# RMSNorm and matmul on one core: tiles 112 to 115 stored as one transfer of four tiles

## The chip, the core and the metric

The kernel runs on one core of one Trainium2 chip. Its time is the device time in microseconds (us) of one launch, and the number compared is the median of several runs. The profile comes from one further execution, whose own time is given beside its span.

## The reference

```python
x: (16, 1024, 512) f32, gamma: (512,) f32, weight: (512, 768) f32
rms = np.sqrt(np.mean(x ** 2, axis=-1, keepdims=True) + eps)
x_norm = x / rms * gamma
return np.matmul(x_norm, weight)          # (16, 1024, 768) f32
```

Flattened, `x` has 16,384 rows (tokens) of 512 numbers and the output has 16,384 rows of 768. The output is 50.33 MB and `x` is 33.55 MB.

## The kernel before

**Tiles.** The tokens are cut into `NT` = 128 tiles of 128 tokens, one token to a partition. Beyond the first 32 tiles the tokens are dealt out so that partition p of a block of 32 tiles holds 32 tokens that follow one another in memory (`rows`, lines 140 to 143). A store of n such tiles therefore writes, for each partition, one run of n x 3,072 bytes: 3,072 bytes for one tile, 9,216 for three, 12,288 for four, 24,576 for eight.

**A tile's way.** `x` is loaded in blocks of 8 tiles (2 MB), cast to bf16 by POOL (L190, L255), turned so that features lie on partitions (PE transposes at L226 and DVE copies at L236; DVE 32 by 32 transposes at L266 for four tiles out of every 16), multiplied by the weights, which already hold gamma (L302, eight matmuls to a tile), and scaled by 1/rms as it leaves PSUM for the buffer `ot`: even tiles by ACT (L274), odd ones by DVE (L276). ACT also sums the squares (L198).

**Order.** `Order` records each operation with what it reads and writes, in program order, and then gives out waits and semaphores. A transfer takes a semaphore from a pool of free ones. The program order is written out by hand in the loop over pairs of tiles (line 420 on).

**Stores.** `ot` has room for 32 tiles. `o_first` and `o_size` (line 138) say which tiles go out together: 4, 4, 8, 8, 8 for the first 32 tiles, then eights, and for the last 32 tiles 8, 8, 1, 3, 4, 4, 3, 1. `finish_tile` calls `store` after each tile; `store` issues a transfer, on SP's queue (line 295), when the tile is the last of its stretch. A stretch whose first tile stands in `DIVIDED` (tile 112 alone) is sent as two transfers, of partitions 0 to 59 and 60 to 127 (`PARTS`). The very last store, of tile 127, is issued by SP after a no-op, while ACT waits for the stores ahead of it (lines 454 to 464).

**What waits for a store.** A slot of `ot` is written again 32 tiles later, so nothing in the kernel writes over tiles 96 to 127 once they are scaled. Their stores are waited for at the end of the program alone. The loads of `x` are issued `LEAD` = 14 pairs ahead, and by the time tile 112 is scaled all of them have landed: after that only stores move.

Of the kernel before, what the change touches and what calls it, by code (L numbers as in the profile page):

```python
# [16 lines left out]
P = 128  # L17
# [83 lines left out]
def kernel(  # L101
# [20 lines left out]
    NT = N // P  # L122
    NP = NT // 2
    XG, RING = 16, 32
# [3 lines left out]
    def stretches(*sizes):  # L128
        first, size, i = {}, {}, 0
        for n in sum(sizes, []):  # L130
            for t in range(i, i + n):
                first[t], size[t] = i, n
            i += n
        assert i == NT
        return first, size

    x_first, x_size = stretches([4, 4, 8, 8, 8], *[[8, 8, 8, 8]] * (NT // RING - 1))
    o_first, o_size = stretches([4, 4, 8, 8, 8], *[[8, 8, 8, 8]] * (NT // RING - 2), [8, 8, 1, 3, 4, 4, 3, 1])

    def rows(ap, i, n):  # L140
        t = 4 if i < 8 else 8 if i < XG else XG if i < RING else RING
        base = i - i % t
        return ap[base * P:(base + t) * P, :].rearrange("(p t) d -> p t d", t=t)[:, i - base:i - base + n, :]
# [26 lines left out]
    def cells(name, slot, i, n=1):  # L170
        return [(name, slot, t) for t in range(i, i + n)]
# [108 lines left out]
    def accumulator():  # L280
        return next(turns) % 3

    DIVIDED = (NT - XG,)
    PARTS = [slice(60), slice(60, P)]

    def store(i):
        first, n = o_first[i], o_size[i]
        if i == first + n - 1:
            at = first % RING
            src, dst = ot[:, at:at + n, :], rows(out, first, n)  # L290
            for part in PARTS if first in DIVIDED else [slice(0, P)]:
                store_rows(dst[part], src[part], cells("ot", 0, at, n) + ([("ot", 1, at + n - 1)] if i == NT - 1 else []))

    def store_rows(dst, src, of):
        order.transfer(SP, lambda: SP.dma_start(out=dst, in_=src), reads=of)
# [23 lines left out]
    def finish_tile(i, a, engine):  # L319
        at = i % RING  # L320

        r = rstd[:, i:i + 1]
        if i == NT - 1:
            for half, by, lo, hi in ((0, ACT, 0, WIDE), (1, DVE, WIDE, O)):
                scale(by, ot[:, at, lo:hi], ops[a][:, lo:hi], r, [("ops", a, half), ("rstd", i)], [("ot", half, at)])
        else:
            before = [("ot", 0, at - 1)] if i == o_first[i] + o_size[i] - 1 and o_size[i] > 1 else []
            scale(engine, ot[:, at, :], ops[a][:, :O], r,
                  [("ops", a, 0), ("ops", a, 1), ("rstd", i)] + before, [("ot", 0, at)] + (opening if i == OPEN else []))
        store(i)  # L330
# [169 lines left out]
```

## The time before, and its profile

| What | Value |
|---|---|
| Median of 3 runs | 208.66 us (208.47 to 208.71) |
| The profiled execution's own time | 208.44 us |
| Its span, first to last instruction | 206.3 us |
| PE busy | 194.7 us, 94% of the span |
| DVE, ACT, POOL busy | 148.4, 145.1, 60.4 us |
| Read from and written to memory | 35.13 MB and 50.33 MB, 414 GB/s over the span |
| Queue 1 (SP: all stores, early loads) | 60.29 MB |
| Queue 10 (ACT: later loads) | 25.17 MB |
| Last matmul ends | about 197.4 us |
| Last store issued | 198.34 us |

The span is measured from the first to the last instruction of the program. The profiled execution took 2.1 us more than its span, and 0.22 us less than the median of the timed runs. An engine of the chip that computes (PE, DVE, ACT, POOL) is told apart from the 16 DMA engines that move the data; the profile's DMA row is the mean busy share of those 16.

### The profile page before, as it was taken

Reading aid. Unit: us, or ns where it says so; the run is one execution under the profiler, and the core shown is the slowest. Engines: PE = TensorE matmul, PEld = TensorE weight load, DVE = VectorE, ACT = ScalarE, POOL = GpSimd, SP = SyncE. Lnnn points to the kernel's source line nnn. Section 1 sums busy time; section 2 is a strip of 40 time slices with the busy share of each in tenths; the row PEclk is TensorE's granted clock in tenths of the full one; section 3 lists DMA queues with packets and bytes.
Section 4 is the critical chain, followed back from the end, with each engine's and each line's share of the span. In section 5 each row is a group of like instructions: output and inputs, shape, how many; then the busy total and the mean of one; then the engine's idle time right before and its main releaser. Section 6 shows DMA issues by size and latency. Waiting matters only on the chain.

```text
span 206.3 us, 2788 instructions
## 1 busy us (share of the span) xinstructions
PE 194.7 (94%) x1240; PEld 72.4 (35%) x717; DVE 148.4 (72%) x254; ACT 145.1 (70%) x345; POOL 60.4 (29%) x36
## 2 busy tenths in 40 slices
PE   7898999999999999999999999999999999999920
PEld 1233443342443333433343333433333334433200
DVE  0445647998579966999579975999569974999500
ACT  2789898877777687777787687677877687663330
POOL 1447733154206430153305170060704215000000
PEclk9999999999999999999999999999999999999985
DMA  6999999999999999999999999999999999999993
GB/s 211 419 438 445 391 392 436 424 447 419 437 424 438 429 427 427 426 442 429 429 429 424 446 426 435 419 422 446 434 429 424 427 432 446 429 415 410 422 421 135
DMA packets 5779, 85.62 MB, mean 415 GB/s; under 512 B 645, under 2 KB 647, under 8 KB 1159
## 3 DMA queue, kind: packets, MB, share of 16 engines
q1 hardware_dynamic: 4035, 60.29, 69.0%
q10 hardware_dynamic: 1732, 25.17, 28.6%
q8 instruction: 7, 0.11, 0.2%
q14 instruction: 5, 0.04, 0.0%
HBM read 35.13 MB, written 50.33 MB: 414 GB/s over the span
## 4 chain that ended last, share of the span: by engine, by line
PE 87%; DMA 7%; SPq 1%; POOL 1%; ACT 0%; issue 0%
PE ps L302 77%; PE ps L226 10%; DMA xt<-in_x_dram 7%; POOL xb L190 1%; SPq L179 1%; SPq L352 0%; ACT ot L274 0%; SPq L495 0%; SPq L454 0%
## 5 line engine op out<-in xcount | busy, mean ns | idle before, releaser
L302 PE MATMUL ps<-w_bf,xT 128*128 128x512 bf16 (+1 forms) x800 | 147.2, 326 | 0.0
L274 ACT ACTIVATE ot<-ps,rstd 128x768 f32<-128x768 f32 (+1 forms) x65 | 58.4, 898 | 47.1 <-PE ps L302 46.1
L198 ACT ACTIVATE jk<-xt 128x512 bf16<-128x512 f32 x128 | 78.7, 619 | 3.0 <-DMA xt<-in_x_dram 3.0
L190 POOL CAST xb<-xt 128x2048 bf16<-128x2048 f32 (+3 forms) x23 | 46.7, 2044 | 105.6 <-PE ps L226 61.7
L276 DVE TENSOR_SCALAR ot<-ps,rstd 128x768 f32<-128x768 f32 x64 | 64.3, 1005 | 10.5 <-PE ps L302 9.1
L298 PEld LDWEIGHTS <-xT 128*128 128x128 bf16 x400 | 39.2, 98 | 58.3 <-issue 57.4
L226 PE MATMUL ps<-ident_f,xb 128*128 128x128 f32 x200 | 54.0, 274 | 1.4 <-POOL xb L190 1.1
L236 DVE COPY xT<-ps 128x1024 bf16<-128x1024 bf16 (+1 forms) x52 | 34.2, 658 | 29.4 <-PE ps L226 28.7
L266 DVE STREAM_TRANSPOSE xTq<-xq 32x256 f32<-32x256 f32 x112 | 48.8, 435 | 1.9
L226 PEld LDWEIGHTS ps<-ident_f,xb 128*128 128x128 f32 x200 | 28.0, 141 | 47.9 <-issue 43.2
L302 PE MATMUL ps<-w_bf,xTq 128*128 128x512 bf16 x224 | 42.8, 326 | 0.0
L198 ACT ACTIVATION_READ_ACCUMULATOR jk<-xt 128x1 f32 x128 | 24.4, 191 | 0.0
L298 PEld LDWEIGHTS <-xTq 128*128 128x128 bf16 x112 | 11.0, 98 | 14.5 <-issue 14.5
L255 POOL CAST xq<-xt 128x2048 bf16<-128x2048 f32 x7 | 13.3, 1897 | 6.1 <-DVE xTq L266 6.1
L302 PE MATMUL ps<-ot 128*128 128x512 bf16 x14 | 5.1, 514 | 1.4 <-DVE ot L360 1.4
L203 ACT ACTIVATE ssq<-ssq,eps_sb 128x8 f32<-128x8 f32 (+3 forms) x20 | 6.0, 299 | 0.5
L205 DVE RECIPROCAL rstd<-ssq 128x8 f32<-128x8 f32 (+3 forms) x20 | 3.7, 191 | 2.7 <-ACT ssq L203 2.7
L274 ACT ACTIVATE w_bf<-ot,g_sb 128x768 bf16<-128x768 f32 x2 | 1.9, 936 | 0.8 <-DMA ot<-in_weight_dram 0.8
L384 DVE COPY g_sb<-ps 128x4 f32<-128x4 f32 x1 | 0.2, 163 | 3.1 <-PE ps L378 3.1
L348 ACT ACT_TABLE_LOAD x1 | 1.3, 1283 | 1.5 <-SPq L454 1.5
L276 DVE TENSOR_SCALAR w_bf<-ot,g_sb 128x512 bf16<-128x512 f32 (+2 forms) x3 | 1.4, 495 | 0.9 <-DMA ot<-in_weight_dram 0.9
L378 PEld LDWEIGHTS ps<-ident_f,ot 2*128 2x128 f32 x2 | 0.3, 200 | 2.6 <-issue 2.6
(11 smaller groups left out, 2.5 us busy)
## 6 DMA issues: line engine op xcount, KB each, us to landing
out_dram<-ot SPq DMA_DIRECT2D x13, 3072.0 KB, 23.2
xt<-in_x_dram ACTq DMA_DIRECT2D x12, 2048.0 KB, 19.2
xt<-in_x_dram SPq DMA_DIRECT2D x3, 2048.0 KB, 18.2
out_dram<-ot SPq DMA_DIRECT2D x4, 1536.0 KB, 9.3
out_dram<-ot SPq DMA_DIRECT2D x2, 1152.0 KB, 9.5
xt<-in_x_dram SPq DMA_DIRECT2D x2, 1024.0 KB, 7.3
ot<-in_weight_dram SPq DMA_DIRECT2D x2, 768.0 KB, 6.3
out_dram<-ot SPq DMA_DIRECT2D x1, 384.0 KB, 7.1
```

The costliest lines, as they stand in the source:

```text
L190: run(POOL, lambda: POOL.tensor_copy(out=xb[s][:, i % 8:i % 8 + n, :], in_=src), of, cells("xb", s, i % 8, n))
L198: run(ACT, lambda: ACT.activation(out=jk[n], in_=src[:, 0, :], func=AF.Square, accum_out=ssq[:, i:i + 1]), of, [("jk", n), ("ssq", i)])
L203: run(ACT, lambda: ACT.activation(out=ssq[:, s], in_=ssq[:, s], func=AF.Sqrt, scale=1.0 / D, bias=eps_sb), [("ssq", t) for t in range(i, i ...
L205: run(DVE, lambda: DVE.reciprocal(out=rstd[:, s], in_=ssq[:, s]), [("rms", i)], [("rstd", t) for t in range(i, i + n)])
L226: run(PE, lambda: PE.transpose(out=tp[b][:, t, h, :], in_=words[:, lo:lo + P], identity=ident_f), cells("xb", s, j % 4 * 2 + t) + ["ident" ...
L236: run(engine, lambda: copy(out=dst[:, t:t + n, :], in_=src[:, t:t + n, :]), [("tp", b)], cells("xT", j % XTS, t, n))
L255: run(POOL, lambda: POOL.tensor_copy(out=xq, in_=src), of, ["xq"])
L266: run(DVE, lambda: DVE.transpose(out=dst, in_=src), ["xq"], [("xTq", n)])
L274: run(ACT, lambda: ACT.mul(out=dst, in_=src, mul=r), reads, writes)
L276: run(DVE, lambda: DVE.tensor_single_scalar(out=dst, in_=src, scalar=r, op=mybir.AluOpType.mult), reads, writes)
L298: run(PE, lambda: PE.ldweights(lhsT), of)
L302: run(PE, lambda: PE.add_instruction(mybir.InstMatmult(name=nc.get_next_instruction_name(), engine=mybir.EngineType.PE, ins=[PE.lower_ap(r ...
```

## The change

Tile 112 joins tiles 113 to 115 in one stretch, and the division by partitions is gone. Where three transfers were issued for these four tiles (60 partitions of tile 112; 68 partitions of tile 112; tiles 113 to 115 on all partitions), one is issued (tiles 112 to 115 on all partitions), after tile 115. The bytes are the same. Nothing else of the kernel is touched.

```diff
-    o_first, o_size = stretches([4, 4, 8, 8, 8], *[[8, 8, 8, 8]] * (NT // RING - 2), [8, 8, 1, 3, 4, 4, 3, 1])
+    o_first, o_size = stretches([4, 4, 8, 8, 8], *[[8, 8, 8, 8]] * (NT // RING - 2), [8, 8, 4, 4, 4, 3, 1])
...
-    DIVIDED = (NT - XG,)
-    PARTS = [slice(60), slice(60, P)]
-
     def store(i):
         first, n = o_first[i], o_size[i]
         if i == first + n - 1:
             at = first % RING
             src, dst = ot[:, at:at + n, :], rows(out, first, n)
-            for part in PARTS if first in DIVIDED else [slice(0, P)]:
+            for part in [slice(0, P)]:
                 store_rows(dst[part], src[part], cells("ot", 0, at, n) + ([("ot", 1, at + n - 1)] if i == NT - 1 else []))
```

## The prediction

> **What bounds the kernel now.** I read the page's slices first. The DMA row stands at 9 from the second slice to the last but one, while PE goes quiet in the last two:
>
> ```profile
> PE   7898999999999999999999999999999999999920
> DMA  6999999999999999999999999999999999999993
> GB/s 211 419 438 445 391 392 436 424 447 419 437 424 438 429 427 427 426 442 429 429 429 424 446 426 435 419 422 446 434 429 424 427 432 446 429 415 410 422 421 135
> ```
>
> PE and the 16 DMA engines are both nearly full, so the end has to be looked at by itself. The chain of waits, cut to the end, stops at the scaling of tile 127 (197.45 us, 0.69 us long). The span goes on to 206.3 us. SP's own waits from 170 us on say what fills the rest:
>
> ```profile
> SPq L295 <- DVE ot L276: 25.2, 4, 10.7
> SPq L495 <- DMA out_dram<-ot: 6.7, 1, 6.7
> SPq L295 <- ACT ot L274: 4.2, 2, 3.4
> ```
>
> L495 is the program's end: it waits 6.7 us for a store. So the last 8 us belong to the stores. The table of stretches shows how (columns: stretch; its length; busy time of PE, PEld, DVE, ACT, POOL; PE clock; DMA share; GB/s):
>
> ```profile
> 187.00:193.00 6.00, 6.00 (x39) 1.76 (x18) 5.07 (x8) 1.80 (x2) 0.00 (x0) 1.00 0.99 415
> 193.00:198.00 5.00, 4.52 (x28) 1.27 (x13) 1.83 (x3) 2.35 (x3) 0.00 (x0) 1.00 0.97 413
> 198.00:202.00 4.00, 0.00 (x0) 0.00 (x0) 0.04 (x1) 0.13 (x1) 0.00 (x0) 0.71 0.99 414
> 202.00:203.20 1.20, 0.00 (x0) 0.00 (x0) 0.00 (x0) 0.00 (x0) 0.00 (x0) 0.50 0.51 207
> 203.20:204.70 1.50, 0.00 (x0) 0.00 (x0) 0.00 (x0) 0.00 (x0) 0.00 (x0) 0.50 0.17 70
> 204.70:206.30 1.60, 0.00 (x0) 0.00 (x0) 0.00 (x0) 0.00 (x0) 0.00 (x0) 0.50 0.01 4
> ```
>
> Full until 202 us, half at 202.6, then a share of 0.17 (three engines of 16) and less. The DMA engines don't end together; a few stragglers set the time, and a change that shifts bytes from one DMA engine to another shifts the end. The three stores that the change merges are three of the page's issues:
>
> ```profile
> out_dram<-ot SPq DMA_DIRECT2D x2, 1152.0 KB, 9.5
> out_dram<-ot SPq DMA_DIRECT2D x1, 384.0 KB, 7.1
> out_dram<-ot SPq DMA_DIRECT2D x1, 204.0 KB
> out_dram<-ot SPq DMA_DIRECT2D x1, 180.0 KB, 14.0
> ```
>
> (one of the two of 1152 KB, and those of 180 and 204 KB.)
>
> To see single engines I went to the trace's landing records. Each DMA engine that takes part in a store adds one to the store's semaphore when its share is down, so a store of all 16 shows 16 times. An engine works its stores off in order, so its landings can be strung together: each lies one share's time behind its landing of the store before.
>
> - Store of 60 rows: one count at 177.98, right at issue, then 15 landings, 187.66 to 191.42. Each lies 0.46 to 0.49 us behind one of the 16 landings of tiles 104 to 111; the landing at 187.99 alone has no follower. So 15 engines carry 4 rows each and one carries none.
> - Store of 68 rows: 12 counts at 178.34, right at issue, then four landings (189.65, 189.72, 191.11, 191.20). Each lies 1.98 to 1.99 us behind a landing of the 60-row store: four engines carry 17 rows each.
>
> The last of the 16 throughout is one engine; I call it X. Its landings beside those of the latest 17-row engine, and of a plain one that never ran dry (us):
>
> ```
> store (tiles)      104-111   60 rows  68 rows  113-115  116-119  120-123  124-126  127
> X                  190.96    191.42   -        194.25   198.01   201.72   204.49   205.41
> 17-row engine      188.75    189.22   191.20   193.95   197.61   201.30   204.02   204.95
> plain engine       189.11    189.58   -        192.32   195.95   199.60   202.36   203.30
> ```
>
> X is the only one that is slower all along: its share of an eight-tile store takes 7.54 us (183.42 to 190.96), where the earliest engine's takes 7.30 (179.89 to 187.19). It takes part in the 60 rows (its 191.42) and not in the 68. It never runs dry: its steps between the last stores, 3.76, 3.71, 2.77 and 0.92 us, are the time of its bytes. The span ends 0.9 us after its last landing.
>
> **The change part by part.**
>
> Bytes per engine. Now X writes 4 rows of 3,072 bytes and 8 of 9,216; afterwards 8 rows of 12,288. That is 12,288 bytes more. The shape after the change is in the trace already, in the two stores behind it (116 to 119, 120 to 123): X needs 3.76 and 3.71 us. What they replace is 0.46 + 2.83 = 3.29 us. The cost is +0.42 to +0.47 us; I take the middle, +0.44. The plain engine confirms it: 3.63 to 3.65 less 0.47 + 2.74 is +0.42 to +0.44. X has no idle time in any step behind this store, so all of it reaches the end: last landing 205.41 + 0.44 = 205.85.
>
> The 17-row engines are relieved. The latest now takes 0.47 + 1.98 + 2.75 = 5.20 us for the four tiles, and would take 3.66: -1.54 us, so it lands last at 203.41. Off the path, because X is later. The plain engines get the same +0.44 and end by 203.74. The engine left out of both parts gets 8 rows more, about 0.9 us, but it ran dry later (its landings of 116-119 and 120-123 lie 4.14 us apart, where 3.65 is work) and ends at 202.35 now; even with all of it, 203.25.
>
> Time of issue. Tile 112's bytes are issued at 182.53 instead of 177.46 and 177.89. What covers this is the eight-tile store ahead, which keeps the first engine busy to 186.8 (its landing, 187.19, less some 0.4 from the last packet's end to its landing). From issue to first packet, an engine that had run dry needed 0.84 us (120-123: issued 193.40, first packet 194.24), so the new transfer is ready at 183.4, 3.4 us ahead. Cost nothing; without the cover it would be up to 5 us on an idle engine.
>
> Issues and waits. SP loses two issues, 0.39 and 0.28 us, and one wait for ACT's tile 112. Its next issue waits for DVE's tile 115 until 182.5 anyway: nothing gained. No wait is added: the merged store waits where the three-tile store waits now. PE, ACT, DVE and POOL keep their instructions, and no slot of `ot` is reused. Per transfer an engine also writes its count, a packet of 0.009 us, one fewer for X; the landing steps already hold it.
>
> A rule of the Trainium skill speaks for the change: "DMA: Bandwidth & Descriptors", section "Rules for kernel authors", says that splitting a transfer by partitions is not worth it, since both halves spray over all 16 engines, and asks for one transfer of 128 partitions. By it the sum would be 0 or slightly below. The trace doesn't bear it out for this split: 15 and 4 landings, not 16 and 16. The same page's rule for the number of engines (section "Why a DMA increments its semaphore by 16 and not by 1": the largest number up to 16 that divides the rows) gives 15 for 60 and 4 for 68, as traced.
>
> **Sum**: +0.44 against the profiled execution, 208.44 to 208.88; the median of the runs is 0.22 higher, so 208.66 + 0.44 = 209.10.
>
> **The rivals.**
>
> 1. *Faster: a 17-row engine sets the end.* If X lands early in the runs that are not profiled, the 17-row engine at 204.95 is last. Without its 17 rows the end falls to the plain engines' 203.74: -1.21 us, 207.45. It decides when X lands before 204.51 (204.95 less 0.44), 0.9 us earlier than traced. For it: X's lead in lateness over that engine is only 0.46 us. Against: X is slower packet after packet over the whole trace, and the timed runs are no shorter than the profiled one, while they would be without X.
>
> 2. *No change: X runs dry first.* Four engines idled some 0.5 us ahead of the store issued at 193.40, and an engine that idles swallows the extra. X would have to be about 3.5 us earlier there (its share of 116-119 lands at 198.01, those four land at 194.07 to 194.39). Time 208.66.
>
> 3. *The last engine is the one left out of both parts.* Then it gains 8 rows, 3.71 to 3.76 less 2.83: +0.9 us, 209.56. In this trace the engine left out is another (187.99 against X's 190.96), and it would need to be the slow one in other runs. The page named above, section "Latency and other measured facts", says that engines 7 and 15 are usually the slower ones, and the one that a 15-engine transfer leaves out is, by its numbering, engine 15; X, which is in the 60 rows and not in the 68, can be 7 and not 15.
>
> That the change doesn't do what it says is hardly open: 8 + 8 + 4 + 4 + 4 + 3 + 1 is 32 tiles, and the store's shape is that of the next two.
>
> **How the numbers follow.** The traced mechanism: 0.72; rival 1: 0.10; rival 2: 0.10; rival 3: 0.08. A measurement of this kernel can tell about 0.2%, 0.42 us, from no change. The forecast's term runs from 0.42 to 0.47, just past it, so a quarter of its chance (0.18) goes to "same" for the scatter of the runs, and 0.54 to "slower". Slower: 0.54 + 0.08 = 0.62; same: 0.18 + 0.10 = 0.28; faster: 0.10. The range runs from 208.5 (rival 2, less the scatter of the runs) to 209.6 (rival 3), and leaves out rival 1.
>
> **What would show it.** In the changed profile: one store of 1536 KB more and none of 180 or 204 KB; its 16 landings between about 190.9 and 194.7; X last there, and last again at about 205.85; the 17-row pair no longer behind the plain engines, so that the stretch from 203.2 us shows fewer stragglers, but a later last one; SP's wait at the end 7.1 instead of 6.7 us. Wrong if X isn't last, if it runs dry, or if its step for the four tiles is not 3.7 us.

## The result, and the profile after

The changed kernel takes 208.83 us (median of 22 runs), the kernel before 208.56 in the same comparison. The ratio of their times is 1.0014 with a 95% interval of 1.0008 to 1.0020: slower by 0.29 us, between 0.17 and 0.42. That is a loss that the interval separates from nothing, and it is under the 0.2% that the prediction set as its bound. The forecast was 209.1 in a range of 208.5 to 209.6.

The profiled execution of the changed kernel took 208.77 us with a span of 206.6. First the slices of its page, and then SP's waits from 170 us on:

```profile
span 206.6 us, 2761 instructions
...
PE   7998999999999999999999999999999999999920
...
DMA  5999999999999999999999999999999999999992
GB/s 205 427 435 438 400 397 431 440 447 425 419 423 431 443 435 420 425 433 435 435 438 422 422 436 433 438 422 417 436 431 438 441 422 427 428 443 402 433 410 96
```

```profile
SPq L292 <- DVE ot L276: 26.7, 4, 10.7
SPq L492 <- DMA out_dram<-ot: 7.0, 1, 7.0
SPq L292 <- ACT ot L274: 3.4, 1, 3.4
```

The body of the kernel is the same: PE and the DMA engines are full, and SP spends the end waiting for the last store. Line 492 is the end that stood at 495 before. Its wait is 7.0 us where it was 6.7, and one of the two waits for ACT is gone, tile 112's. The table of stretches at the end (columns as before: stretch; its length; busy time of the five engines; PE clock; DMA share; GB/s):

```profile
198.00:202.00 4.00, 0.00 (x0) 0.00 (x0) 0.04 (x1) 0.13 (x1) 0.00 (x0) 0.91 0.99 414
202.00:203.20 1.20, 0.00 (x0) 0.00 (x0) 0.00 (x0) 0.00 (x0) 0.00 (x0) 0.50 0.48 195
203.20:204.70 1.50, 0.00 (x0) 0.00 (x0) 0.00 (x0) 0.00 (x0) 0.00 (x0) 0.50 0.06 27
204.70:206.60 1.90, 0.00 (x0) 0.00 (x0) 0.00 (x0) 0.00 (x0) 0.00 (x0) 0.50 0.02 6
```

The stretch from 203.2 to 204.7 shows the change: a DMA share of 0.06, one engine of 16, where it was 0.17, three engines. Two stragglers have gone; the one that is left works on longer, and moves 6 GB/s instead of 4 behind 204.7. The issues of stores:

```profile
out_dram<-ot SPq DMA_DIRECT2D x5, 1536.0 KB, 10.8
...
out_dram<-ot SPq DMA_DIRECT2D x1, 1152.0 KB, 7.6
out_dram<-ot SPq DMA_DIRECT2D x1, 384.0 KB, 7.4
```

Five stores of 1536 KB instead of four, one of 1152 instead of two, none of 180 or 204. The landing records of the slow engine, X, as before (us):

```
store (tiles)      104-111   112-115  116-119  120-123  124-126  127
X                  190.80    194.55   198.32   202.03   204.78   205.72
latest of others   188.92    192.56   196.19   199.82   202.59   203.50
```

X's step over the four tiles is 3.75 us, and no engine is within 2.2 us of it at the end.

### The profile page after: what moved, and what is told of

It is laid out like the page before. It is cut to its first block, busy times and chain, and to the rows that moved or that the text cites. A ratio compares the mean times of both kernels' runs of the same rounds, so it can differ in the third digit from the quotient of the medians.

```text
span 206.6 us, 2761 instructions
## 1 busy us (share of the span) xinstructions
PE 194.0 (94%) x1216; PEld 72.4 (35%) x717; DVE 148.3 (72%) x254; ACT 145.1 (70%) x345; POOL 60.4 (29%) x36
## 4 chain that ended last, share of the span: by engine, by line
PE 86%; DMA 7%; SPq 1%; POOL 1%; issue 1%; ACT 0%
PE ps L299 76%; PE ps L226 10%; DMA xt<-in_x_dram 7%; POOL xb L190 1%; SPq L179 1%; SPq L349 0%; ACT ot L274 0%; SPq L492 0%; SPq L451 0%
## 5 line engine op out<-in xcount | busy, mean ns | idle before, releaser
L299 PE MATMUL ps<-w_bf,xT 128*128 128x256 bf16 (+1 forms) x783 | 144.5, 325 | 0.9
L299 PE MATMUL ps<-w_bf,xTq 128*128 128x256 bf16 (+1 forms) x217 | 41.8, 324 | 0.4
L299 PE MATMUL ps<-ot 128*128 128x512 bf16 x14 | 5.9, 576 | 1.4 <-DVE ot L357 1.4
```

The costliest lines, as they stand in the source:

```text
L299: run(PE, lambda: PE.add_instruction(mybir.InstMatmult(name=nc.get_next_instruction_name(), engine=mybir.EngineType.PE, ins=[PE.lower_ap(r ...
```

## The experiments

Times are told as the ratio to the kernel before on the same chip, with its 95% interval; 0.001 is 0.21 us. A diff is against the kernel before unless it says otherwise.

**Tile 112 whole, the rest as it was** (undivided).

```diff
-    DIVIDED = (NT - XG,)
+    DIVIDED = ()
```

> Tile 112 goes out whole, as one transfer of 128 partitions at its old time, and tiles 113 to 115 as before. Bytes theory (the time follows the bytes that the last DMA engine, X, has to write): X again writes 8 rows of tile 112 instead of 4, as after the change, so the time is that of the changed kernel, 0.29 to 0.44 us over the kernel before (208.85 to 209.0), X's landings end about 205.8. Rival, joining: the loss comes from making one transfer out of three (later issue, one long run per partition): then the time stays with the kernel before, 208.56.

Ratio 1.0009 (0.9994 to 1.0024), which by itself tells neither theory from the other. The landings do: X takes 190.73 to 191.67 for tile 112 (0.94 us for 8 rows, where 4 took 0.46) and lands last at 205.65. So the extra bytes came with the division's removal, although nothing was merged.

**The three transfers kept, all issued after tile 115** (late_issue).

```diff
+        if i == 115:
+            store_stretch(112)
+        if i != 112:
+            store_stretch(i)
...
-                store_rows(dst[part], src[part], cells("ot", 0, at, n) + ([("ot", 1, at + n - 1)] if i == NT - 1 else []))
+                store_rows(dst[part], src[part], cells("ot", 0, at, n) + ([("ot", 1, at + n - 1)] if i == NT - 1 else []) + (cells("ot", 0, 115 % RING) if first == 112 else []))
```

> The three transfers stay (60 and 68 rows of tile 112, then tiles 113 to 115), but all are issued after tile 115, as the merged one is. Bytes theory: the same rows on the same engines and the queue ahead covers the later issue, so 208.56, no change (within 0.1 us). Rival, late issue: the 5 us by which tile 112 is issued later are what costs, so 208.85, the time of the changed kernel.

Ratio 0.9990 (0.9977 to 1.0004). The 60 rows were issued at 182.67 us, the 68 at 183.12, and their first landings are at 187.51 and 189.52 as in the profile before (187.66, 189.65). The queue ahead covers 5 us of later issue, and the last landing is 205.45. Late issue is not the cost. Between this kernel and the one with tile 112 whole, run together on one chip, lies 0.0019, 0.40 us (runs of 208.35 to 208.78 against 208.67 to 209.36; an interval for this pair is not on record).

**Four tiles at 60 and 68 partitions** (four_at_60_68; the diff is against the changed kernel).

```diff
-            for part in [slice(0, P)]:
+            for part in [slice(60), slice(60, P)] if first == 112 else [slice(0, P)]:
```

> The four tiles are stored together but divided at 60 and 68 partitions, rows of 12288 bytes. Bytes theory: X has 4 rows instead of 8, 1.9 us less, and is not last; the four engines that carry 4 + 17 rows need 9.6 us where 3.65 are needed now, so they end about 209.4 instead of 203.5 on the landing scale and set the time, 3.7 us over the changed kernel: 212.6. Rival, every transfer is spread over all 16 engines: 208.8, no change.

219.19 us in one run: the direction that the bytes gave, and nearly three times the loss (10.4 us over the changed kernel where 3.7 were expected). X has its 4 rows in 1.86 us and is far from last; the four engines with 17 rows land them at 198.70, 202.86, 203.25 and 205.17, and the last of these sets the end, 216.17. 17 rows at 0.46 us are 7.8 us; the first has that, the others needed more. The table of stretches of this kernel, and then the kernel before in its stretch of the same name:

```profile
190.00:199.00 9.00, 7.57 (x47) 2.16 (x22) 4.14 (x6) 3.39 (x4) 0.00 (x0) 1.00 0.99 325
199.00:203.00 4.00, 0.00 (x0) 0.00 (x0) 0.00 (x0) 0.00 (x0) 0.00 (x0) 0.68 0.93 323
```

```profile
190.00:199.00 9.00, 7.52 (x47) 2.15 (x22) 4.04 (x6) 3.39 (x4) 0.00 (x0) 1.00 1.00 425
```

The DMA engines are as busy (0.99 against 1.00) and move 325 GB/s instead of 425. In the packet records of this run 70 of the 384 packets of 12,288 bytes behind 185 us took over 0.8 us, where the median is 0.46; the profiles of the kernel before and of the changed kernel have none. So these packets seem to have been held back by something else than an engine's own pace. That part of my expectation was wrong; what it is that they share was not tried, and there is one run and one profile of it.

**Tile 112 in parts of 119, 8 and 1** (parts_119_8_1).

```diff
-    PARTS = [slice(60), slice(60, P)]
+    PARTS = [slice(119), slice(119, 127), slice(127, P)]
```

> Stretches as before, tile 112 divided into 119, 8 and 1 partitions: by the counting that 60 and 68 showed (the largest number up to 16 that divides the rows), on 7, 8 and 1 engines. Bytes theory: X has 1 row of tile 112 if it is the eighth engine, none if it is a later one, 18 if it is one of the first seven. With 1 row X ends 7 x 0.117 = 0.82 us ahead of the changed kernel and the first seven, with 18 rows each, end at about 204.7, just ahead of X: 208.0, faster than both kernels. With 18 rows on X: 210.0. The landings of the 8-row part tell which. Rival, one transfer is best and each further one costs: 208.9 or more.

Ratio 1.0064 (1.0043 to 1.0086). X is in the part of 119: its landing follows the one of tiles 104 to 111 by 2.05 us, 17 rows (190.95, 193.00), and it has a row of the part of 8 as well (193.20). With 18 rows it lands last at 207.04. My hope that X was the eighth engine was wrong; the 210.0 that I gave for the other case was the median, 210.04.

**Parts of 114 and 14, and of 115 and 13** (parts_114_14 and parts_115_13).

```diff
-    PARTS = [slice(60), slice(60, P)]
+    PARTS = [slice(114), slice(114, P)]      # the other: slice(115), slice(115, P)
```

> Tile 112 divided into 114 and 14 partitions: 6 engines with 19 rows each, and 14 engines with 1 row each. Parts of 119, 8 and 1 showed that X is one of the first seven and 60 and 68 that it isn't one of the first four. If X is the seventh: 1 row instead of 4, X ends 0.35 us earlier than before, at 205.06, the first six have 20 rows and the latest of them end at about 203.3 + 12 x 0.117 = 204.7; time 208.2, faster than both kernels. If X is the fifth or sixth: 20 rows, 16 x 0.117 = 1.87 us later, 210.4. Rival, a tile is best stored whole and each part costs: 208.7 to 209.

> Tile 112 divided into 115 and 13 partitions: 5 engines with 23 rows each, and 13 engines with 1 row each. If X is the sixth or seventh: 1 row, X ends at 205.06; the first five have 24 rows and the latest of them end at about 203.3 + 16 x 0.117 = 205.2 and set the time, 208.3 to 208.4. If X is the fifth: 24 rows, 20 x 0.117 = 2.3 us later than before, 210.9.

Ratios 1.0089 (1.0075 to 1.0102) and 1.0103 (1.0088 to 1.0119). In both, X is in the large part: 2.26 us for 19 rows, and 2.74 us for 23, the second with five engines only. It wasn't in the four of the 68 rows. So X is the fifth engine, in the order in which these parts fill them. Within each kernel that has two parts, the engines of the smaller group landed rows of both (here five of the 13 landings lie 0.18 to 0.20 us behind the five of the large part); that the order is the same from kernel to kernel is taken, not shown. The parts that tell the fifth ran on one chip; on the chip of the 119 rows X is among the first seven and not among the four. The times, 210.35 and 210.72, are the ones written for that case (210.4 and 210.9).

**Both kernels once more** (before_again and after_again), unchanged.

> The kernel before once more, unchanged. Both theories: ratio 1.000 within the scatter of the runs. It shows how far X's lateness ahead of tile 112 (its landing of tiles 104 to 111, 190.96 in the first profile) differs between profiles of one kernel: if by 0.1 to 0.2 us, then the difference between the 0.44 us of the sum and the 0.27 us between the medians is scatter; if not at all, the sum is too high for another reason.

> The changed kernel once more, unchanged. Bytes theory: X's four steps from its landing of tiles 104 to 111 to its last are 14.9 us again, where the kernel before shows 14.45, so the sum's term of 0.44 to 0.47 holds, and the runs give between 0.2 and 0.5 us over the kernel before. Rival, the change costs less than its term because X works faster with whole transfers: steps of 14.7 us or less.

Ratios 1.0001 (0.9992 to 1.0011) and 1.0023 (1.0013 to 1.0033): this time the changed kernel is slower by 0.48 us, between 0.27 and 0.69. X's landing of tiles 104 to 111 was at 191.24 in this execution of the kernel before, 0.28 us later than in the first one, with the steps behind it the same, 14.46 us. So how late X stands ahead of tile 112 differs by a few tenths between executions of the same kernel, and the change's own term doesn't. In these two profiles the last landings lie only 0.11 us apart, and the steps behind tiles 104 to 111 0.44: one execution against another can't tell this change, medians of many can.

**Two tiles divided** (two_divided).

```diff
-    ... [8, 8, 1, 3, 4, 4, 3, 1])
+    ... [8, 8, 1, 3, 1, 3, 4, 3, 1])
...
-    DIVIDED = (NT - XG,)
+    DIVIDED = (NT - XG, NT - XG + 4)
```

> Two tiles divided at 60 and 68 partitions, 112 and 116 (116 alone, then 117 to 119). Bytes theory: X is spared 4 more rows and would end 0.45 us earlier than before (204.96), but the 17-row engines carry 13 more rows, 1.53 us, and end at 206.5; they set the time now, 1.07 us over the kernel before: 209.6. Rival, X alone sets the time whatever the others carry: 208.1.

Ratio 1.0078 (1.0058 to 1.0097), 1.6 us. The profile is as expected: the 17-row pair is last, at 206.47 and 206.61, some 1.6 us behind X. The profiled execution took 209.64, the number written; the other timed runs took 210.02 to 210.65. Why they took up to a microsecond more was not found. This is the prediction's first rival made real: where X is spared enough, those who carry its rows set the end.

**Parts of 48, 76 and 4** (parts_48_76_4).

```diff
-    PARTS = [slice(60), slice(60, P)]
+    PARTS = [slice(48), slice(48, 124), slice(124, P)]
```

> Tile 112 divided into 48, 76 and 4 partitions (16 engines with 3 rows, 4 with 19, 4 with 1). Bytes theory: X has 3 rows instead of 4 and ends 0.12 us earlier than before; the first four have 23 rows instead of 21 and end 0.23 us later, still just ahead of X: 0.12 us faster than before, 208.44, about the least that can be had by this lever. Rival, every further part costs a fixed time of some tenths: 208.7 or more.

Ratio 0.9991 (0.9982 to 0.9999). X lands last at 205.57, 14.35 us behind its landing of tiles 104 to 111 (14.45 before), and the pair with the most rows is at 205.15 and 205.26. It is faster than the kernel before by 0.19 us, where 0.12 were expected, and the one kernel here whose interval leaves out no change on that side, only just. The row that X is spared accounts for 0.10 us; the rest can be scatter.

**Tile 112, and tiles 112 and 113, from POOL's queue** (pool_one_tile and pool_two_tiles).

```diff
-                free = [k for k, d in enumerate(slots) if known[at].get(("transfer", d), 0)]
+                free = [k for k, d in enumerate(slots) if engine is not nc.gpsimd and known[at].get(("transfer", d), 0)]
...
-    PARTS = [slice(60), slice(60, P)]
+    PARTS = [slice(5), slice(5, 126), slice(126, P)]
...
-                store_rows(dst[part], ...
+                store_rows(POOL if first in DIVIDED else SP, dst[part], ...
...
-    ... [8, 8, 1, 3, 4, 4, 3, 1])
+    ... [8, 8, 2, 2, 4, 4, 3, 1])            # the second kernel alone
```

> Tile 112 is stored from POOL's queue in 5, 121 and 2 partitions; the rest as before. X is the fifth engine (23 rows in the parts 115 and 13). If a transfer from POOL goes on with the engine after the last one used, 5 rows fall on the first five engines and 121 on the other eleven, 11 rows each: X has 1 row instead of 4 and ends 0.35 us earlier, at 205.06, and nobody else is near: 208.2. If it starts at the first engine each time, X has 1 + 11 rows, 0.94 us more: 209.5. A rival: POOL's way of issuing adds its own time ahead of the transfer, which the queue hides, or at the program's end, which it doesn't: then above 208.6 with X's landings as in the first case. The Trainium skill, DMA: Bandwidth & Descriptors, section Why a DMA increments its semaphore by 16 and not by 1, says the first case for this queue.

> As pool_one_tile, with tiles 112 and 113 in rows of 6144 bytes (5, 121 and 2 partitions from POOL's queue), and 114 and 115 as one store of all partitions. If the engines are dealt out in turn, X writes 2 row-pairs fewer than nearly all others: 1 x 2 + 8 x 2 rows of 3072 for the four tiles instead of 32 in the changed kernel, 14 x 0.117 = 1.64 us less, 204.1; the eleven others have 6 rows more, 0.7 us, 204.2. All end together, and the time is 207.3, 1.25 us faster than before. If it starts at the first engine each time, X has 22 + 2 instead of 16 rows of the two tiles: 209.8.

Ratios 1.0025 (1.0011 to 1.0038) and 1.0058 (1.0038 to 1.0078): slower, and X's rows went by neither of the two ways written. The queues of the first, from the window in which tile 112 goes out (queue, kind: packets, MB, share of the 16 engines):

```profile
## 3 DMA queue, kind: packets, MB, share of 16 engines
q1 hardware_dynamic: 288, 4.25, 90.3%
q0 software_dynamic: 144, 0.39, 8.9%
```

POOL's transfers run as a queue of their own, q0, beside SP's q1, and are served in turn with it: the packets lie between those of tiles 104 to 111 from 182 us on. In the packet records 60 packets of q0 are 6,144 bytes long, two rows each: read as four, eight rows, on each of 15 engines, and the row that is left on the sixteenth. X's share of tiles 104 to 111, with which they mix, took 8.31 us instead of some 7.5, so X is taken to be one of the 15. It was spared nothing: it lands last at 206.29 and 206.14. Eight rows alone would have put it at about 205.7, as in undivided. What holds the other 0.6 us (a row of the part of 5, if X has one, is 0.1) was not tried, nor why the span ends 1.3 us behind the last landing here and 0.9 elsewhere; the third way written, that issuing from POOL adds time of its own, is therefore open. The Trainium skill, "DMA: Bandwidth & Descriptors", section "Why a DMA increments its semaphore by 16 and not by 1", names just this exception to its rule of counting (on trn2, some copies from POOL go over 16 engines, each with the number of partitions divided by 16 and rounded up, which is 8 for 121); I had written the rule and not the exception.

## Why the prediction was right, and where it wasn't

**The step that carried it holds.** One table sets the number of rows of tile 112 on X against the time from X's landing of tiles 104 to 111 to its last landing, and against a line of 14.45 us plus 0.1165 us for each row over four, drawn through the rows for 4 and 24:

```
kernel            rows on X   landings of X       us      line
parts_48_76_4          3      191.22   205.57     14.35   14.33
before                 4      190.96   205.41     14.45   14.45
before_again           4      191.24   205.70     14.46   14.45
late_issue             4      190.99   205.45     14.46   14.45
undivided              8      190.73   205.65     14.92   14.92
after                  8      190.80   205.72     14.92   14.92
after_again            8      190.91   205.81     14.90   14.92
parts_119_8_1         18      190.95   207.04     16.09   16.08
parts_114_14          20      191.03   207.36     16.33   16.31
parts_115_13          24      191.06   207.84     16.78   16.78
```

In these ten profiles X is the last to land, and the time follows its rows to 0.02 us; neither the number of transfers (one to four for these tiles), nor their lengths of row, nor when they were issued enters. The change gives X four rows, 0.44 to 0.47 us, where the prediction had 0.42 to 0.47.

**The rest of the sum.** The four tiles' step was to be 3.71 to 3.76 us and was 3.75 and 3.74 in the two profiles. The 17-row pair was to leave the end, and the plain engines to land by 203.74: the latest lands at 203.50 in the first profile; in the second, one engine that was late already ahead of tile 112 lands at 204.39, still 1.42 us ahead of X. The later issue was to cost nothing, and late_issue shows that. SP's last wait was to be 7.1 us and is 7.0. The last landing was to be 205.85 and was 205.72 and 205.81.

**What was mis-sized.** Between the medians of the first comparison lies 0.27 us and by its ratio 0.29, two thirds of the 0.44 that the sum gave, and "slower by over 0.2%" had the most chance where "within 0.2%" came out. The weak step is the last one, the sum against one profiled execution: it took X's lateness at tile 112 as a given of the kernel. It differs between executions: 190.73 to 191.24 us in these ten profiles, 190.96 and 191.24 for one and the same kernel. In the first two profiles it took back 0.16 us of the 0.47, in the second two 0.33 of the 0.44. It stands ahead of anything the change touches: X's landing of tiles 88 to 95 is at 175.87 and 175.73 us in the first two profiles and at 176.17 and 175.84 in the second two, and the first issue that differs is the one at 177.46. The second comparison gave 0.48 us and the pair of undivided and late_issue 0.40, and both agree with 0.44; the interval of the first comparison ends at 0.42, just short of it. What makes the first one smaller is not shown. It can be chance; but in each of the three comparisons that have both, the kernels that store tile 112 whole had X at tiles 104 to 111 earlier than the others, by 0.12 us at least, and whether that goes with the kernels is open. A quarter for "same" was too little for a term that lay on the bound itself; that single runs of the kernel before differ by some 0.2 us could have been read off its three runs (208.47 to 208.71).

**The rivals.** A 17-row engine setting the end didn't happen here and does where two tiles are divided. X running dry didn't happen. The third rival, that the last engine is the one left out of both parts, didn't happen: X has a landing of the 60 rows in every profile with that division of tile 112 (191.39 to 191.73). There I leaned on the Trainium skill's remark on engines 7 and 15 ("DMA: Bandwidth & Descriptors", section "Latency and other measured facts"), which the page ties, as a best guess, to descriptors written for POOL's transfers, and this kernel has none of these. I wrote that X can be 7; by the same numbering the parts of 115 and 13 exclude 7. The rule of the same page's "Rules for kernel authors", one transfer rather than two by partitions, would have made the change free or a gain; the runs don't bear it out for parts of 60 and 68, which don't fall on the same engines.

## What to carry to other kernels

At the end of a kernel that is full of transfers, look at the DMA engines one by one: the landing records of a store, one for each engine, show who is last, and only that engine's bytes move the end. How a transfer's partitions divide decides which engines carry it, so a division by 60 and 68 is a choice of engines and not of size; it pays until those that take the rows over become the last. A term of two thousandths is to be held against the scatter of what the sum starts from before it is given as a change that can be told.

## What the runs showed of the hardware that was not expected

- One DMA engine is slower than the others in every profile here, and it is the fifth where the parts tell which: 7.51 to 7.57 us for its share of a 3 MB store in the profiles without transfers from POOL, where others take 7.2 to 7.3. It stands some 2 us behind the plain ones by the end. This is read from landings, share by share; the packet records name no engine, so the prediction's "packet after packet" is not shown.
- Where four engines had 17 rows of 12,288 bytes each, the DMA engines moved 325 GB/s at a busy share of 0.99, and 70 packets took over 0.8 us instead of 0.46. With rows of 3,072 bytes the same division, in the kernel before, had 425 GB/s and no such packet. The cause is open.
- A store from POOL's queue of 121 partitions was spread over all 16 engines in packets of two rows, where one of 119 partitions from SP's queue used seven engines.
